# A two-block attention kernel: 64-row products padded to 128 rows, and x, meta tokens and norm weights also passed with features on the partitions

## The chip, the cores and the metric

The kernel runs on one core of a Trainium2 chip. The metric is the device time of one execution, in microseconds. Before the change it is 1644.33 us, the median of three runs (1641.67 to 1646.13).

## The reference

512 tokens of 2048 features pass through two blocks in float32. The first is sliding-window attention with sinks: 32 query heads of 64 share 4 key and value heads, each query sees 128 positions, and a learned bias by distance is added. Put short:

```
h = rms_norm(x, swa_norm);  q, k, v, gate = split(h @ w_in)          # 2048 x 4608
p = softmax with sink (q_norm . k_norm / 8 + bias, window 128)
x = x + ((p @ v) * silu(gate)) @ w_out
```

The second puts 16 meta tokens ahead of the sequence (528 positions) and runs two kinds of causal attention side by side, 8 heads each, on one normalised input. Differential heads ("d" in the code) have two 64-wide halves of q and k, a penalty linear in distance, and subtract one softmax from the other. Latent heads ("m") have q, k and v projected from narrow normalised latents plus a rotary part.

```
h = concat(meta_tokens, x);  proj = rms_norm(h, attn_norm_w) @ w_in
d: w = softmax(q0 k0' / 8 - slope*dist) - lam * softmax(q1 k1' / 8 - slope*dist);  o = rms_norm(w @ v)
m: o = softmax((q_nope k_nope' + q_pe k_pe') / sqrt(192)) @ v
h = h + (concat(o_d, o_m) * silu(gates)) @ w_out;  y = rms_norm(h, final_norm)[16:]
```

## The kernel before

Every large product is made at nearly float32 precision out of three float32r products: both operands are split into a rounded high part and the low rest, and high x high, high x low and low x high are accumulated in PSUM. ScalarE makes high parts (`wh` at L158, others in `split`, L268), VectorE the low ones (`wl` at L168, others at L272 and L274). Weights stream from HBM in 512 KB pieces (`Weights`, three raw buffers, up to four units of high and low parts ahead).

The work goes in stages: the first block's k and v projection (`kv_ps`, 16 steps over k, four token tiles each), its four q projections with attention pieces mixed in, its gates, its output projection; then the second block's latents, the heads, gates and output projection. In the head stage `Flow` counts units (three or so projection products each) and lets attention pieces in between: `s1` makes a block's scores, `norm` normalises, `s2` transposes the probabilities (L1304), `s2b` handles the last 16 columns of a block, `s3` multiplies by the values. There are 16 heads with four query blocks each.

The order of ScalarE, TensorE and VectorE is as written in the first k and v projection; later mostly ScalarE's alone (`phase({ACT})`), and a planner with its own cost estimates places the others. DMA issues, all on SyncE's queue, and GpSimd are always the planner's.

The first k and v projection needs x with features on the partitions. x is loaded with tokens on the partitions, in column blocks (`xc`), and `x_to_t` (L423) makes four TensorE transposes (L427) a step, after which `split` scales by the norm weight in `gcols` and rounds. `gcols`, 39 columns of norm weights, is itself made by transposing rows (`grow`). The sum of squares is taken by ScalarE (`squares`, L420), summed at k = 13 and turned into `rstd1` by two GpSimd operations (`rsqrt_mean`, L106 and L108); the evacuations of the four `kv_ps` banks (L549, L268, L274) need it. The next projection takes the same four banks. Ten warm-up transposes stand ahead of the transposes of x, and five behind the first four (L409).

In `s1` a differential head's scores are two products a half (L1253, L1254). The 128-row one pairs `dq` with the high and low parts of k stacked; the 64-row one adds the low part of q times the high part of k:

```
r = slice(64 * comp, 64 * comp + 64)
mm(o, qh[comp][:, qs], kh[comp][:, a:b], True, False)
mm(o, ql[r, qs], kh[comp][r, a:b], False, True)
```

`ql` is one tile (`dql`) whose upper half belongs to comp 0 and the lower to comp 1. Blocks 0 to 2 have one column range, block 3 has two. A latent head makes five 128-row products in the same place (`mqh`, `mql`, `mkh`, `mkl`, `qpt`, `kph`, `kpl`).

Because 528 positions are four tiles and 16 columns, each block's last 16 columns are collected in an edge tile of 64 rows (four blocks of 16). `s3` ends with three products over these 64 rows (L1342 to L1344: `pbh`, `pbl`, with the value rows `vh[:64, 4]`, `vl[:64, 4]`). The edge rows of the values come from products with 64 output rows (`mla_proj`) or from one transpose of 64 output rows (`te`, L1211), those of the probabilities from another (`edge`, L1323).

The second block's meta tokens are loaded as 16 rows and transposed by 16 products (`mps`, L847).

Of the kernel before, what the change touches and what calls it, by code (L numbers as in the profile page):

```python
# [9 lines left out]
F32 = mybir.dt.float32  # L10
# [8 lines left out]
KT = 16  # L19
# [16 lines left out]
def mixer_kernel(ctx, tc, x, rel_bias, swa_norm, w_in1, q_gain, k_gain, sinks, w_out1,  # L36
                 meta, attn_norm, w_in2, dlam, subln, qnorm, w_uq, kvnorm, w_ukv, w_out2,
                 fnorm, c_hot, c_out, c_rel, c_mask, c_cos, c_sin, out):
# [336 lines left out]
    def load_x(c, parts=1):  # L375
        t = xs.tile([128, NTB, 512], F32, tag="x", name="xcol", bufs=3)
        n = 512 // parts
        for i in range(parts):
            o = c * 512 + i * n
            nc.sync.dma_start(out=t[:, :, i * n:(i + 1) * n],  # L380
                              in_=x[:, o:o + n].rearrange("(t p) c -> p t c", p=128))
        return t

    grow = xs.tile([39, 128], F32, name="grow")

    def load_g(r, ap):
# [55 lines left out]
    def misc_a():  # L442
        for r, ap in ((16, attn_norm), (32, qnorm), (36, kvnorm), (38, subln)):
            load_g(r, ap)
# [15 lines left out]

    def misc_c():
        gps = tpt()
        nc.tensor.transpose(gps[:, 0, :39], grow, ident[:39, :39])
        nc.vector.tensor_copy(out=gcols[:, 16:39], in_=gps[:, 0, 16:39])
# [21 lines left out]
    for c in range(1, 3):  # L486
        xc.append(load_x(c))
# [6 lines left out]
    for k in range(KT):  # L494
# [5 lines left out]
        if k == 11:  # L500
            misc_c()
# [1089 lines left out]
```

## Time and profile before

| what | before |
|---|---|
| median of three runs | 1644.33 us |
| the profiled execution's own time / its span | 1643.65 / 1641.9 us |
| TensorE matmul busy, instructions | 1628.0 us (99%), 8674 |
| TensorE weight loads busy | 1373.1 us (84%) |
| VectorE / ScalarE / GpSimd busy | 906.9 (55%) / 731.8 (45%) / 86.5 (5%) us |
| mean granted TensorE clock | 0.999 |
| DMA | 173.65 MB, mean 106 GB/s |

PE is TensorE, PEld its weight loads, DVE VectorE, ACT ScalarE, POOL GpSimd, SPq the queue that issues the DMAs. In the timeline a row starts with its start and its duration in us, and rows of one kind that follow each other are merged (x4), their duration being that of all; a matmul's duration includes the pipeline's length, so rows overlap. A form such as `64*128 64x264` is a product over 64 rows with 128 output rows, moving 264 columns. A bracket at a row's end tells how long the engine sat idle before it and what ended that.

### The profile page before, as it was taken

How to read it: one execution, taken by the hardware profiler on the slowest of the kernel's cores; microseconds unless marked ns; L12 is line 12 of the kernel's file. 1: busy time of each engine (PE TensorE's matmuls, PEld its weight loads, DVE VectorE, ACT ScalarE, POOL GpSimd, SP SyncE). 2: the span in 40 equal slices, each digit the busy share in tenths (PEclk: the TensorE clock that was granted, in tenths of full speed). 3: DMA queues.
4: the chain of work that ended last, by engine and by line, in shares of the span. 5: the costliest groups of instructions: out<-in, count | busy, mean ns of one | idle time of the engine just before them, and what ended most of it. 6: DMA issues, size and time to landing. Idle time of an engine off the chain costs nothing.

```text
span 1641.9 us, 23349 instructions
## 1 busy us (share of the span) xinstructions
PE 1628.0 (99%) x8674; PEld 1373.1 (84%) x8674; DVE 906.9 (55%) x2220; ACT 731.8 (45%) x1624; POOL 86.5 (5%) x145
## 2 busy tenths in 40 slices
PE   9999999999999999999999999999999999999998
PEld 7888888887888888889898898898898788888887
DVE  4548888896444333333765656656556455455332
ACT  6456776774333332233554444444444333334222
POOL 0130320200000000000100000000000000000000
PEclk9999999999999999999999999999999999999999
DMA  7422323225434433333322222132132274355212
GB/s 226 134 86 81 104 85 99 81 59 176 125 94 126 159 117 137 103 119 81 84 75 71 65 82 75 56 84 71 55 90 71 72 224 123 96 218 180 91 51 103
DMA packets 145488, 173.65 MB, mean 106 GB/s; under 512 B 12967, under 2 KB 83406, under 8 KB 144846
## 3 DMA queue, kind: packets, MB, share of 16 engines
q1 hardware_dynamic: 145374, 172.16, 34.1%
q8 instruction: 68, 1.11, 0.3%
q14 instruction: 46, 0.38, 0.1%
HBM read 155.28 MB, written 16.84 MB: 105 GB/s over the span
## 4 chain that ended last, share of the span: by engine, by line
PE 94%; DVE 3%; ACT 2%; DMA 1%; issue 0%; POOL 0%; SPq 0%; ACTq 0%; POOLq 0%; DVEq 0%
PE pj L111 79%; PE sc L111 6%; PE pv L111 4%; PE tp L708 1%; PE tp L1304 1%; PE tp L427 1%; PE tp L636 1%; DMA oin<-ot_d 0%; PE sqs L1358 0%; PE ck_m L111 0%; ACT p L683 0%; DVE wl L168 0%; DMA xcol<-in_x_dram 0%; PE xtp L427 0%; DVE dk L272 0%
## 5 line engine op out<-in xcount | busy, mean ns | idle before, releaser
L168 DVE TENSOR_TENSOR wl<-raw,wh 128x512 fp32r<-128x512 f32 (+1 forms) x488 | 329.5, 682 | 421.4 <-ACT wh L158 419.3
L158 ACT ACTIVATE wh<-raw 128x512 fp32r<-128x512 f32 (+1 forms) x488 | 298.8, 619 | 405.6 <-PE pj L111 360.2
L111 PE MATMUL pj<-xh,wh 128*128 128x512 f32 (+1 forms) x1152 | 368.1, 356 | 0.0
L111 PE MATMUL pj<-xh,wl 128*128 128x512 f32 (+1 forms) x1152 | 356.5, 345 | 0.6 <-DVE wl L168 0.6
L111 PE MATMUL pj<-xl,wh 128*128 128x512 f32 (+1 forms) x1152 | 356.3, 345 | 0.0
L111 PEld LDWEIGHTS pj<-xh,wh 128*128 128x128 f32 x1152 | 204.7, 188 | 34.6 <-issue 3.1
L111 PEld LDWEIGHTS pj<-xh,wl 128*128 128x128 f32 x1152 | 199.7, 188 | 27.6 <-DVE wl L168 1.1
L111 PEld LDWEIGHTS pj<-xl,wh 128*128 128x128 f32 x1152 | 199.9, 188 | 19.7
L111 PE MATMUL pj<-wh,ogh 128*128 128x512 f32 (+1 forms) x528 | 205.0, 388 | 0.0
L111 PE MATMUL pj<-wh,ogl 128*128 128x512 f32 (+1 forms) x528 | 203.9, 386 | 0.0
L111 PE MATMUL pj<-wl,ogh 128*128 128x512 f32 (+1 forms) x528 | 203.8, 386 | 0.0
L111 PE MATMUL pj<-wh,xh 128*128 128x512 f32 (+1 forms) x448 | 176.8, 395 | 0.0
L111 PE MATMUL pj<-wh,xl 128*128 128x512 f32 (+1 forms) x448 | 171.2, 382 | 0.0
L111 PE MATMUL pj<-wl,xh 128*128 128x512 f32 (+1 forms) x448 | 170.8, 381 | 0.0
L1267 ACT ACTIVATE p2t<-p2t,nm 128x144 f32<-128x144 f32 (+3 forms) x96 | 55.2, 575 | 152.3 <-DVE nm L1263 152.2
L111 PEld LDWEIGHTS pj<-wh,ogl 128*128 128x128 f32 x528 | 99.3, 188 | 21.2
L111 PEld LDWEIGHTS pj<-wl,ogh 128*128 128x128 f32 x528 | 99.4, 188 | 20.6
L111 PEld LDWEIGHTS pj<-wh,ogh 128*128 128x128 f32 x528 | 99.3, 188 | 20.5
L111 PEld LDWEIGHTS pj<-wh,xl 128*128 128x128 f32 x448 | 84.4, 188 | 16.2
L111 PEld LDWEIGHTS pj<-wl,xh 128*128 128x128 f32 x448 | 84.7, 189 | 11.4
L111 PEld LDWEIGHTS pj<-wh,xh 128*128 128x128 f32 x448 | 84.5, 189 | 11.3
L683 ACT ACTIVATE p<-p,nm 128x256 f32<-128x256 f32 (+1 forms) x128 | 60.7, 476 | 60.6 <-DVE nm L679 60.5
(313 smaller groups left out, 2077.7 us busy)
## 6 DMA issues: line engine op xcount, KB each, us to landing
raw<-in_swa_w_in_dram SPq DMA_DIRECT2D x72, 512.0 KB, 3.6
raw<-in_w_in_dram SPq DMA_DIRECT2D x56, 512.0 KB, 3.7
raw<-in_swa_w_out_dram SPq DMA_DIRECT2D x32, 512.0 KB, 3.8
raw<-in_w_in_dram SPq DMA_DIRECT2D x128, 128.0 KB, 2.5
raw<-in_w_out_dram SPq DMA_DIRECT2D x32, 512.0 KB, 3.6
oin<-ot_d SPq DMA_DIRECT2D x8, 1024.0 KB, 7.3
bias<-bm_d SPq DMA_DIRECT2D x8, 512.0 KB, 5.3
ot_d<-ot SPq DMA_DIRECT2D x32, 128.0 KB, 1.8
```

Of the source, the lines that this page charges most:

```text
L111: nc.tensor.matmul(o, lhsT=l, rhs=r, start=start, stop=stop)
L158: nc.scalar.activation(out=h[:, :n], in_=self.raw_t[r][:, o:o + n], func=ACTF.Copy)
L168: nc.vector.tensor_tensor(out=l[:, :n], in0=self.raw_t[r][:, o:o + n], in1=f32(h[:, :n]), op=ALU.subtract)
L427: nc.tensor.transpose(tp[:, t, :], xcol[:, t, i * 128:(i + 1) * 128], ident)
L636: nc.tensor.transpose(tp[:, h, :].bitcast(F32R), qs[:, 4 * i + h].rearrange("p a b -> p (a b)"), identr)
L683: nc.scalar.activation(out=p[:, b, :w], in_=p[:, b, :w], func=ACTF.Exp, scale=-1.0, bias=nm[:, b:b + 1], accum_out=sm[:, b:b + 1])
L708: nc.tensor.transpose(tp[:, b, :], st[n]["p"][:, b, kb * 128:(kb + 1) * 128], ident)
L1267: nc.scalar.activation(out=p[:, :w], in_=p[:, :w], func=ACTF.Exp, scale=-1.0, bias=m, accum_out=sums[:, comp:comp + 1])
L1304: nc.tensor.transpose(tp[:, kb, :], p[:, kb * 128:(kb + 1) * 128], ident)
```

## The change

- Inputs: x is given a second time as `x_t` [2048, 512], the meta tokens as `meta_t` [128, 16, 16], and the five small norm weights as `gains` [128, 39]; the host lays them out. The row forms of the norm weights are no longer inputs.
- First k and v projection: `gcols` is one DMA. `x_t` is loaded into one tile `xt` in six pieces, four ahead of the loop and two at k = 1 and 2. `x_split(k)` scales and rounds out of SBUF; no transposes. `x_square(k)` squares on ScalarE and GpSimd adds up into `acc`; at k = 15 four products of `acc` with a column of ones give the sums. Warm-up: 30 transposes in a row.
- Meta tokens: `mps` is loaded, not transposed.
- Edges: all edge tiles have 128 rows or columns, zeros behind the 64. `ql` becomes two persistent tiles, each with one half zero, and all products in `s1`, `s3` and `mla_proj` take 128 rows.
- `dynamic_dma_scratch_size=4096` in the program's set-up.

```diff
-    def load_x(c, parts=1):
-        t = xs.tile([128, NTB, 512], F32, tag="x", name="xcol", bufs=3)
-        n = 512 // parts
-        for i in range(parts):
-            o = c * 512 + i * n
-            nc.sync.dma_start(out=t[:, :, i * n:(i + 1) * n],
-                              in_=x[:, o:o + n].rearrange("(t p) c -> p t c", p=128))
-        return t
-
-    grow = xs.tile([39, 128], F32, name="grow")
-
-    def load_g(r, ap):
-        n = ap.shape[1] // 128
-        nc.sync.dma_start(out=grow[r:r + n, :], in_=ap[0].rearrange("(k p) -> k p", p=128))
-
-    load_g(0, swa_norm)
-    xc = [xs.tile([128, NTB, 512], F32, tag="x", name="xcol", bufs=3)]
-    for i, (a, b) in enumerate(((0, 128), (128, 256), (256, 512))):
-        nc.sync.dma_start(out=xc[0][:, :, a:b], in_=x[:, a:b].rearrange("(t p) c -> p t c", p=128))
-        if i % 2 == 0:
-            W.load(i // 2)
+    nc.sync.dma_start(out=gcols, in_=gains)
+    xt = xs.tile([128, KT, S], F32, name="xt")
+
+    def load_xt(a, b):
+        nc.sync.dma_start(out=xt[:, a:b, :], in_=x_t[a * 128:b * 128, :].rearrange("(k p) c -> p k c", p=128))
+
+    load_xt(0, 1)
+    W.load(0)
+    load_xt(1, 2)
+    load_xt(2, 4)
+    W.load(1)
     W.nr = 2
+    load_xt(4, 7)
...
-    warm_up(10)
-    gps = tpt()
-    nc.tensor.transpose(gps[:, 0, :16], grow[:16], ident[:16, :16])
-    nc.vector.tensor_copy(out=gcols[:, 0:16], in_=gps[:, 0, :16])
-
-    ss1 = xs.tile([128, NTB, 4], F32, name="ss1")
+    warm_up(30)
+
+    acc = xs.tile([128, S], F32, name="acc")
+
+    def x_split(k):
+        split(xh1[:, k, :], xl1[:, k, :], xt[:, k, :], gcols[:, G1 + k:G1 + k + 1])
+
+    def x_square(k):
+
+        sq = acc if k == 0 else xs.tile([128, S], F32, tag="xsq", name="xsq", bufs=3)
+        nc.scalar.activation(out=sq, in_=xt[:, k, :], func=ACTF.Square)
+        if k:
+            nc.gpsimd.tensor_tensor(out=acc, in0=acc, in1=sq, op=ALU.add)
...
-    sq_done = set()
-    for c in range(1, 3):
-        xc.append(load_x(c))
-    x_to_t(xc[0], 0, 0, xh1, xl1, 0, G1)
+    x_split(0)
     W.high(0)
-    warm_up(5)
     F.run_posts()
     W.low(0)
-    x_to_t(xc[0], 0, 1, xh1, xl1, 0, G1, True)
+    x_split(1)
     for k in range(KT):
+        if k == 1:
+            load_xt(7, 12)
         if k == 2:
-            xc.append(load_x(3))
+            load_xt(12, 16)
             mi = misc_a()
         if k == 10:
             misc_b(*mi)
-        if k == 11:
-            misc_c()
         F.run_posts()
         W.get(c_kv, k)
         wh, wl = W.get(c_kv, k)
-        nx = k + 2
-        if 2 < nx < KT:
-            x_to_t(xc[nx // 4], nx // 4, nx % 4, xh1, xl1, 0, G1, nx % 2 == 1)
-        if 0 < k < 12:
-            for q in range(min(16, k * 4 // 3 + 2)):
-                if q not in sq_done:
-                    sq_done.add(q)
-                    squares(xc[q // 4], q // 4, ss1, xs, q % 4)
-        if k == 13:
+        if k + 2 < KT:
+            x_split(k + 2)
+        for q in range(KT):
+            if k > 0 and (k - 1) * 5 // 4 <= q < k * 5 // 4:
+                x_square(q)
+        if k == KT - 1:
+            ssp = ps_sc.tile([128, 512], F32, tag="sc", name="ssp")
+            for t in range(NTB):
+                nc.tensor.matmul(ssp[:, 2 * t:2 * t + 2], lhsT=acc[:, t * 128:(t + 1) * 128], rhs=ones2,
+                                 start=True, stop=True)
             ssr = xs.tile([128, NTB], F32, name="ssr")
-            nc.vector.tensor_reduce(out=ssr, in_=ss1, axis=AX.X, op=ALU.add)
+            nc.vector.tensor_copy(out=ssr, in_=ssp[:, 0:8].rearrange("p (a b) -> p a b", b=2)[:, :, 0])
             rsqrt_mean(rstd1, ssr, D)
...
-            if k == 0 and b == 1:
-                x_to_t(xc[0], 0, 2, xh1, xl1, 0, G1)
...
+        mps = xr_p.tile([128, KT, 16], F32, name="mps")
+        nc.sync.dma_start(out=mps, in_=meta_t)
...
-            mps = ps_tp.tile([128, KT, 16], F32, tag="tp", name="mps")
-            for k in range(KT):
-                nc.tensor.transpose(mps[:, k, :], mt[:, k * 128:(k + 1) * 128], ident[:16, :16])
...
-        CW = 2 * LK + 128
+        CW = 2 * LK + 256
         B2["ckh"] = ms.tile([128, CW], F32R, name="ckh")
         B2["ckl"] = ms.tile([128, CW], F32R, name="ckl")
+        for n_ in ("ckh", "ckl"):
+            nc.gpsimd.memset(f32(B2[n_][:, 2 * LK:]), 0.0)
...
-        B2["edge"] = [B2["p2"].tile([128, 64], F32, name=f"edge{i}") for i in range(2)]
-        for t in B2["edge"]:
+        B2["edge"] = [B2["p2"].tile([128, 128], F32, name=f"edge{i}") for i in range(2)]
+        B2["te"] = B2["p2"].tile([128, 128], F32, name="te")
+        B2["qlz"] = [B2["p2"].tile([128, S], F32R, name=f"dql{i}") for i in range(2)]
+        for t in B2["edge"] + [B2["te"]] + [f32(q) for q in B2["qlz"]]:
...
-                            c = slice(2 * LK + 64 * k, 2 * LK + 64 * k + 64)
+                            c = slice(2 * LK + 128 * k, 2 * LK + 128 * k + 128)
                             ah, al = B2["ckh"][:, c], B2["ckl"][:, c]
-                            o = o[:64]
...
-            ql = p2.tile([128, S], F32R, tag="dql", name="dql", bufs=1)
+            ql = B2["qlz"]
...
-                split(qd[i][half[i]], ql[half[i]], t[half[i], :S])
+                split(qd[i][half[i]], ql[i][half[i]], t[half[i], :S])
...
-                nc.tensor.transpose(tp[:64, 0, :], te, ident)
-                split(vh[:64, 4], vl[:64, 4], tp[:64, 0, :])
+                nc.tensor.transpose(tp[:, 0, :], te, ident)
+                split(vh[:, 4], vl[:, 4], tp[:, 0, :])
...
-                    r = slice(64 * comp, 64 * comp + 64)
                     mm(o, qh[comp][:, qs], kh[comp][:, a:b], True, False)
-                    mm(o, ql[r, qs], kh[comp][r, a:b], False, True)
+                    mm(o, ql[comp][:, qs], kh[comp][:, a:b], False, True)
...
-            nc.tensor.transpose(tp[:64, 0, :], pe, ident)
-            split(hd["pbh"], hd["pbl"], tp[:64, 0, :].rearrange("p (j c) -> p j c", j=4)[:, :, 16:32])
+            nc.tensor.transpose(tp[:, 0, :], pe, ident)
+            split(hd["pbh"], hd["pbl"], tp[:, 0, :].rearrange("p (j c) -> p j c", j=4)[:, :, 16:32])
...
-            mm(oc, vh[:64, 4, :], pbh, False, False)
-            mm(oc, vh[:64, 4, :], pbl, False, False)
-            mm(oc, vl[:64, 4, :], pbh, False, True)
+            mm(oc, vh[:, 4, :], pbh, False, False)
+            mm(oc, vh[:, 4, :], pbl, False, False)
+            mm(oc, vl[:, 4, :], pbh, False, True)
...
+def _columns(inputs):
+
+    import numpy as np
+    x_t = np.ascontiguousarray(np.asarray(inputs["x"])[0].T)
+    m = np.asarray(inputs["meta_tokens_2"])
+    meta_t = np.ascontiguousarray(m.reshape(META, KT, 128).transpose(2, 1, 0))
+    names = ("swa_norm", "attn_norm_w_2", "mla_q_norm_w_2", "mla_kv_norm_w_2", "diff_subln_w_2")
+    gains = np.concatenate([np.asarray(inputs[n])[0].reshape(-1, 128) for n in names])
+    return [("x_t", x_t), ("meta_t", meta_t), ("gains", np.ascontiguousarray(gains.T))]
...
-    nc = _bacc.Bacc("TRN2", target_bir_lowering=False, num_devices=1)
+    nc = _bacc.Bacc("TRN2", target_bir_lowering=False, num_devices=1, dynamic_dma_scratch_size=4096)
```

## Rows read from the trace of the kernel before

**Rows 1.** The page's chain that ended last, its shares by engine.

```profile
PE 94%; DVE 3%; ACT 2%; DMA 1%; issue 0%; POOL 0%; SPq 0%; ACTq 0%; POOLq 0%; DVEq 0%
```

**Rows 2.** Timeline of TensorE, latent scores: start us, duration us, engine, line, operation, names, form.

```profile
842.31 0.29 PE L111 MATMUL sc<-mkh,mql 128*128 128x264 f32 x1
842.43 0.29 PE L111 MATMUL sc<-kph,qpt 128*128 128x264 f32 x1
```

**Rows 3.** Timeline of all engines, the first projection's end.

```profile
57.73 0.39 PE L111 MATMUL pj<-wh,xh 128*128 128x512 f32 x1
...
58.67 0.47 ACT L549 ACTIVATE kn_all<-pj,rstd 128x256 f32<-128x256 f32 x1
...
59.60 0.48 DVE L274 SCALAR_TENSOR_TENSOR v<-pj,rstd,v 128x256 fp32r<-128x256 f32 x1 [0.31 <-ACT v L268]
...
60.45 0.39 PE L111 MATMUL pj<-wh,xh 128*128 128x512 f32 x1
```

**Rows 4.** Timeline of TensorE, one differential half.

```profile
863.61 0.28 PE L111 MATMUL sc<-dk,dq 128*128 128x272 f32 x1
863.83 0.39 PE L111 MATMUL sc<-dk,dql 64*128 64x272 f32 x1
864.15 0.50 PE L111 MATMUL pj<-xh,wh 128*128 128x512 f32 x1
864.48 0.39 PE L111 MATMUL pj<-xl,wh 128*128 128x512 f32 x1
```

**Rows 5.** View by tile, dql: count, durations min/median/max in ns, forms.

```profile
L111 PE MATMUL sc<-dk,dql x80: 379/387/449, 850.2 to 1297.3; 64*128 64x264 f32 x32, 64*128 64x256 f32 x16, 64*128 64x272 f32 x16, 64*128 64x400 f32 x16
```

**Rows 6.** Timeline of TensorE, end of one head's value sum.

```profile
866.27 0.28 PE L111 MATMUL pv<-pth,mvl 128*128 128x256 f32 x1
...
866.61 0.27 PE L111 MATMUL pv<-pbl,mvh 64*128 64x64 f32 x1
866.72 0.27 PE L111 MATMUL pv<-pbh,mvl 64*128 64x64 f32 x1
...
867.27 0.39 PE L111 MATMUL pj<-xl,wh 128*128 128x512 f32 x1
```

**Rows 7.** Timeline of TensorE, the meta tokens.

```profile
536.34 0.39 PE L111 MATMUL pj<-wh,ogl 128*128 128x512 f32 x1
536.65 1.16 PE L847 MATMUL mps<-identr,mt 16*128 16x16 f32 x16
537.74 0.50 PE L111 MATMUL pj<-wh,ogh 128*128 128x512 f32 x1
```

**Rows 8.** Timeline of TensorE, one step of the first projection.

```profile
24.98 0.60 PE L427 MATMUL xtp<-identr,xcol 128*128 128x128 f32 x4
...
28.17 0.60 PE L427 MATMUL tp<-identr,xcol 128*128 128x128 f32 x4
```

**Rows 9.** Timeline of all engines, the start.

```profile
1.63 2.39 PE L409 MATMUL pj<-identr 128*128 128x128 f32 x10 [1.63 <-DVE identr L404]
...
6.20 0.63 ACT L158 ACTIVATE wh<-raw 128x512 fp32r<-128x512 f32 x1 [0.19 <-DMA raw<-in_swa_w_in_dram]
...
7.82 0.78 PE L111 MATMUL pj<-wh,xh 128*128 128x512 f32 x1
...
8.39 0.63 PE L111 MATMUL pj<-wl,xh 128*128 128x512 f32 x1
...
10.10 0.43 PE L111 MATMUL pj<-wh,xl 128*128 128x512 f32 x1
```

**Rows 10.** View by windows: busy us (count) by engine, clock, DMA share, GB/s.

```profile
8.00:10.00 2.00, 2.00 (x6) 1.62 (x6) 1.08 (x2) 1.21 (x2) 0.00 (x0) 1.00 1.05 390
```

**Rows 11.** View by lines, GpSimd: busy us, mean ns, idle before.

```profile
L626 POOL TENSOR_TENSOR qn<-qn,st 128x512 f32<-128x512 f32 x16 | 17.8, 1111 | 1.3
...
L108 POOL TENSOR_TENSOR rstd<-rstd,mhalf 128x4 f32<-128x4 f32 x2 | 2.0, 1020 | 0.2
```

**Rows 12.** View by lines and forms, TensorE: busy us, mean ns, idle before, releaser.

```profile
L1304 PE MATMUL tp<-identr,p2t 128*128 128x128 f32 x160 | 28.1, 274 | 0.9 <-DVE p2t L1283 0.6
```

More of the change, by code (lines that the diff above doesn't have):

```diff
@@ L35, in mixer_kernel @@
 @with_exitstack
-def mixer_kernel(ctx, tc, x, rel_bias, swa_norm, w_in1, q_gain, k_gain, sinks, w_out1,
-                 meta, attn_norm, w_in2, dlam, subln, qnorm, w_uq, kvnorm, w_ukv, w_out2,
-                 fnorm, c_hot, c_out, c_rel, c_mask, c_cos, c_sin, out):
+def mixer_kernel(ctx, tc, x, rel_bias, w_in1, q_gain, k_gain, sinks, w_out1,
+                 meta, w_in2, dlam, w_uq, w_ukv, w_out2, fnorm,
+                 x_t, meta_t, gains, c_hot, c_out, c_rel, c_mask, c_cos, c_sin, out):
     nc = tc.nc
@@ L442, in misc_a @@
     def misc_a():
-        for r, ap in ((16, attn_norm), (32, qnorm), (36, kvnorm), (38, subln)):
-            load_g(r, ap)
         srow = xs.tile([128, 32], F32, name="srow")
@@ L459, in misc_a @@
         return srow, gq_t, gk_t, relt, hot, outm, lrow
[L461 to L464, printed above, removed]
     def misc_b(srow, gq_t, gk_t, relt, hot, outm, lrow):
@@ L1018, in edges @@
             for nm_ in ("ckh", "ckl"):
-                e = B2[nm_][:, 2 * LK + 64 * k:2 * LK + 64 * k + 64]
+                e = B2[nm_][:, 2 * LK + 128 * k:2 * LK + 128 * k + 64]
                 nc.vector.tensor_copy(out=e.rearrange("p (j c) -> p j c", j=4),
@@ L1142, in mla_proj @@
                     F.unit()
-                n = 128 if b0 < 4 else 64
-                split(vh[:n, b0:b0 + nb].rearrange("p a b c -> p (a b c)"),
-                      vl[:n, b0:b0 + nb].rearrange("p a b c -> p (a b c)"), pv[:n, :nb * 256])
+                split(vh[:, b0:b0 + nb].rearrange("p a b c -> p (a b c)"),
+                      vl[:, b0:b0 + nb].rearrange("p a b c -> p (a b c)"), pv[:, :nb * 256])
         vh, vl = heads["v"]
@@ L1215, in ev @@
             F.defer(3, tr2)
-            te = p2.tile([128, 64], F32, tag="te", name="te", bufs=1)
+            te = B2["te"]
             F.post(lambda: nc.vector.tensor_copy(
-                out=te.rearrange("p (j c) -> p j c", j=4), in_=edge(t)))
+                out=te[:, 0:64].rearrange("p (j c) -> p j c", j=4), in_=edge(t)))
         proj_t(c_dv[h], KT, [(slice(0, 128), [(pk[i][:, :HALF], hv[i]) for i in range(2)], ev)])
@@ L1292, in s2 @@
                     ptl=p2.tile([128, PTW], F32R, tag="ptl", name="ptl2", bufs=1),
-                    pbh=p2.tile([64, 4, 16], F32R, tag="pbh", name="pbh", bufs=1),
-                    pbl=p2.tile([64, 4, 16], F32R, tag="pbl", name="pbl", bufs=1))
+                    pbh=p2.tile([128, 4, 16], F32R, tag="pbh", name="pbh", bufs=1),
+                    pbl=p2.tile([128, 4, 16], F32R, tag="pbl", name="pbl", bufs=1))
             hd = st[kind, h]
@@ L1578 @@
     from concourse.bass_utils import run_bass_kernel_spmd as _run
-    nc = _bacc.Bacc("TRN2", target_bir_lowering=False, num_devices=1)
+    nc = _bacc.Bacc("TRN2", target_bir_lowering=False, num_devices=1, dynamic_dma_scratch_size=4096)
     arrays, args = {}, []
-    pairs = [(n, _np.ascontiguousarray(inputs[n])) for n in _INS] + _constants()
+    pairs = [(n, _np.ascontiguousarray(inputs[n])) for n in _INS] + _columns(inputs) + _constants()
     for name, a in pairs:
```

5 lines of the change are left out of this document (2 added, 3 removed).

## The prediction

> **What bounds the kernel now.** I read the chain of waits first: TensorE holds nearly all of it [rows 1], so the span is the sum of what TensorE does, and other engines count only where TensorE waits for them. Its busy time says little here, because matmuls are pipelined and a row's duration overlaps the next one. The price of a product is its slot: from its own start to the start of the next row in the timeline. A 264-column product of 128 rows takes 0.12 us [rows 2]; twelve 512-column products take 2.72 us (57.73 to 60.45), 0.23 each [rows 3]. The reader should look for places where a slot is longer than the column count explains. There are three kinds, and the change touches them all.
>
> **The 64-row score products.** In a differential head each block of scores is a 128-row product (dq) and a 64-row product (dql). The stretch dq, dql, next projection product takes 0.87 us, 863.61 to 864.48 [rows 4]. At full-row prices it would be 0.12 + 0.12 + 0.23, with a trifle for 272 columns: 0.48. The excess is 0.39: the slot before the 64-row product is 0.22 instead of 0.12, its own 0.32 instead of 0.12, the one after it 0.33 instead of 0.23. The latent heads make five 128-row products in a row beside the same projections, and their slots are the plain 0.12 [rows 2]; so what is dear is going into 64 rows and out again. The change gives ql 128 rows, one half of them zero. There are 80 such products [rows 5]: 80 x 0.39 = 31.2 us off the path. Columns and weights loaded stay as they are. Bounds: at best all 31.2; at worst nothing, if the slot belongs to these operands and not to the row count. I take 31.2, since the nearest full-row products of the same width show no excess.
>
> The Trainium skill speaks against it (TensorE: Matmul & The Clock Gate, "Why this matters for your kernels"): a small-K product takes the same time as a 128-row one, and the gain lies in running several at once on distinct row groups. By that the padding is worth nothing, and the sum is some 6 us. The trace disagrees, with 0.32 against 0.12 for the slot. It is a rival below.
>
> **The 64-row edge products.** Each of 16 heads ends its sum of probabilities by values with three 64-row products of 64 columns. From the last 128-row product ahead of them to the second product behind, 866.27 to 867.27, are 1.00 us [rows 6]. Plain: 0.12 for 256 columns, 0.23 for 512, and three times 0.11, the slot of the middle one (866.61 to 866.72), which changes no mode: 0.68. Excess 0.32; I take 0.31, as some are followed by shorter products: 16 x 0.31 = 5.0 us. Bounds 0 and 5.1. Products whose output has 64 rows (the value edges, the transposes of te and edge) also become 128 wide. Their moving columns don't change, so I take nothing; if the wider weight load showed, it would be at most half of a 0.11 slot for each of 24 transposes, 1.3 us. The new zero fills lie on GpSimd, idle there, once, under projection products ahead of the first head's scores.
>
> **Meta tokens.** Sixteen transposes of 16 rows go: 536.65 to 537.74 is 1.09 us, the slot ahead of them is 0.31 instead of 0.23 [rows 7], and leaving the mode costs 0.10 as in rows 4. That is 1.3 us. The transfer that replaces them is issued 20 units ahead of its use.
>
> **The first projection.** x arrives with features on the partitions, so 16 groups of four transposes go. One step over k takes 3.19 us with a group, 24.98 to 28.17 [rows 8], and 2.72 without [rows 3]: 0.47 a group. Fourteen lie behind the slow start: 6.6 us. The first two belong to the start, which I price as a whole.
>
> The start: the first projection product begins at 7.82, four slots of 0.43 run from 8.39 to 10.10 [rows 9], and later ones take 0.23 [rows 3]. TensorE runs at the lower of its two levels, 1.2 GHz, in that stretch, although the view by windows gives 1.00 for its clock [rows 10]. After the change the first product needs the first weights, rounded at 6.20 + 0.63 = 6.83 [rows 9], and the end of thirty warm-up transposes instead of fifteen. Ten take 2.39 us [rows 9], so thirty end near 8.0 at the lower level. If the clock doesn't rise in them, the first product starts 0.2 late and its half-speed successors cost the 1.1 us of before: about zero. If it rises in them, products start at 6.9 at full speed; less 0.4 for VectorE's first low half, 1.7 us are won. If it rises 3 us later than now, 1.7 are lost. I take zero, since the fifteen transposes did not raise it before the products came.
>
> The Trainium skill has the same of transposes (TensorE: Matmul & The Clock Gate, Part 4): they don't count as busy in the same way; by it the upper end, 1.7 us won, falls away. No run here shows thirty without a pause.
>
> Transfers: the first pass takes x and weights of 4.2 MB each, and TensorE needs 16 x 2.72 = 44 us for it; a full queue moves 390 GB/s [rows 10], 22 us for both. The weights for k = 6, with all the x queued ahead of them, are 5.2 MB, 14 us of transfer, wanted some 23 us into the span. No loss.
>
> The sum of squares moves from accumulating activations to plain squares on ScalarE and 15 adds on GpSimd at 1.11 us [rows 11], 17 us beside 35 us of products: hidden. But its last step moves to the beginning of k = 15: four tiny products on TensorE (priced as four slots of 0.11 and one change of mode at 0.08: 0.5), a copy, then the power on GpSimd, 1.02 us [rows 11]; with the small operation ahead of it and the handovers some 2.0 from the last product's step. The first evacuation now begins 0.94 after the step's start (58.67 against 57.73) and frees its bank at 59.60 + 0.48 = 60.08, 0.37 ahead of the next projection at 60.45 [rows 3]. After the change it begins about 2.0 after that start, 1.06 later: TensorE waits 0.7. Behind it on ScalarE are the other seven evacuations and weight halves that are three units ahead; the second bank is wanted six products later, with over a microsecond to spare. Loss 0.5 + 0.7. The stage wins 6.6 - 1.2 = 5.4 us, with the start's bounds 3.7 to 7.1.
>
> **What is late next.** Shorter scores leave VectorE and ScalarE less time before the transposes of the probabilities. TensorE sits idle ahead of these for 0.9 us in all 160 now [rows 12]. At worst one in four of the 64 query blocks loses a saved 0.39: 6.2 us; at best none. I take 1.5, near the present 0.9.
>
> **Sum.** 31.2 + 5.0 + 1.3 + 5.4 - 1.5 = 41.4. The profiled execution took 1643.65 us (span 1641.9 and 1.75 around it): 1602.2. It lies 0.7 under the median of the runs, 1644.33; I forecast 1602.5.
>
> **Rivals.**
> 1. The padded products keep their long slots. Only meta tokens and the first stage pay, 1.3 + 5.4: 1637. For it: dq and dql alternate operands. Against: so do the latent scores, at 0.12. Chance 0.05.
> 2. The softmax chain takes half of the 36 us of scores and edges back, because transposes then wait for the normalisation: 1620. For it: one releaser, the normalisation, ended 0.6 of the 0.9 us [rows 12]. Against: that is small over 160. It decides from 0.3 us a block. Chance 0.10.
> 3. Slower: in the attention stage only ScalarE keeps the written order, so the planner may place VectorE's normalisation so late that the transposes of every one of the 64 blocks wait for it. From 42.9 / 64 = 0.67 us a block the gain is gone; at 0.8 the time is 1643.65 - 42.9 + 51.2 = 1652. For it: waits of this kind exist [rows 12]. Against: the change adds nothing to VectorE's chain there, so a wait can mostly only return what was saved. Chance 0.03.
>
> The forecast has the remaining 0.82.
>
> **Numbers.** The forecast's own range: the start 1.7 either way, edge transposes 1.3, returned waits up to 4.7 more, another order by the planner some 2: 1597 to 1612. With a little of rival 2's side the range is 1596 to 1614. A difference of 0.3%, 5 us, is what can be told from none. Faster: the forecast and rivals 1 and 2 but for 0.02: 0.95; same 0.02; slower 0.03.
>
> **What would show it.** Right: slots of dq and dql both 0.12; the first projection at 2.7 us a step and its end near 55; under 1 us of waiting ahead of the second projection; more idle time ahead of the transposes of the probabilities. Wrong: padded products with 0.3 us slots; TensorE idle on x or weights in the first 30 us; blocks whose transposes wait regularly.

## The result, and the profile after

| | before | after |
|---|---|---|
| median of four runs each, us | 1643.51 (1641.67 to 1646.13) | 1604.52 (1603.41 to 1606.12) |
| ratio to before, 95% interval | | 0.9762 (0.9745 to 0.9779) |
| profiled execution, us | 1643.65 | 1604.56 |
| its span, us | 1641.9 | 1602.8 |

Of the executions below, one (of the run with the later broadcast) took 7605.23 us and is left out. The forecast was 1602.5 us, in a range from 1596 to 1614. The time lies 2.0 us above it. To find where that comes from, I cut both spans at the same points of the written order (the first product of each stage), so that every stage has its own difference:

| stage | before | after | won | forecast |
|---|---|---|---|---|
| span's start to the first projection's first product | 7.82 | 6.47 | 1.35 | 0 (with the slow slots behind it) |
| first projection, to the second one's first product | 52.64 | 49.81 | 2.83 | 5.4 |
| first output projection, with the meta tokens (to its last three products) | 185.55 | 185.09 | 0.46 | 1.3 |
| first to last dql product | 447.11 | 413.12 | 33.99 | |
| last dql to the second output projection | 161.11 | 160.52 | 0.59 | |
| the last two lines together (the heads) | | | 34.58 | 31.2 + 5.0 - 1.5 = 34.7 |
| all other stages together | | | -0.1 | 0 |

The heads came as forecast; the first projection and the meta tokens gave less.

**The whole.** The chain that ended last by engine, of after [rows 1]:

```profile
PE 91%; DVE 4%; ACT 2%; DMA 1%; issue 1%; POOL 0%; SPq 0%; ACTq 0%; POOLq 0%; DVEq 0%
```

TensorE still sets the end. Its share falls by three points, which is more than the 39 of 1642 us that went: the chain now passes through VectorE in more places. Which waits became longer is read stage by stage below.

**The score products.** TensorE's timeline over one differential half of after [rows 4]; columns as there:

```profile
852.33 0.29 PE L111 MATMUL sc<-dk,dq 128*128 128x272 f32 x1
852.46 0.29 PE L111 MATMUL sc<-dk,dql 128*128 128x272 f32 x1
852.58 0.39 PE L111 MATMUL pj<-xh,wh 128*128 128x512 f32 x1
852.81 0.40 PE L111 MATMUL pj<-xl,wh 128*128 128x512 f32 x1
```

The view by tile, dql [rows 5]:

```profile
L111 PE MATMUL sc<-dk,dql x80: 278/284/349, 845.8 to 1258.9; 128*128 128x264 f32 x32, 128*128 128x256 f32 x16, 128*128 128x272 f32 x16, 128*128 128x400 f32 x16
```

From dq to the second projection product are 0.48 us now, 0.87 before. The reader should compare starts, not durations: dql's own duration fell by only 0.1 us, its slot by 0.20.

**The edges.** TensorE's timeline at the end of one head's value sum [rows 6]:

```profile
860.37 0.28 PE L111 MATMUL pv<-pth,mvl 128*128 128x256 f32 x1
860.48 0.19 PE L111 MATMUL pv<-pbh,mvh 128*128 128x64 f32 x1
860.51 0.27 PE L111 MATMUL pv<-pbl,mvh 128*128 128x64 f32 x1
...
860.73 0.48 PE L111 MATMUL pj<-xh,wh 128*128 128x512 f32 x1
861.05 0.39 PE L111 MATMUL pj<-xl,wh 128*128 128x512 f32 x1
```

0.68 us from the first to the last of these rows, 1.00 before. That is the figure worked out in the prediction, but its terms are not: the first edge product's slot is 0.03 and not 0.11, and the projection product behind takes 0.32 and not 0.23. That the two deviations cancel in this head is luck.

**The transposes of the probabilities.** View by lines and forms [rows 12]:

```profile
L1290 PE MATMUL tp<-identr,p2t 128*128 128x128 f32 x160 | 28.0, 273 | 1.9 <-DVE p2t L1269 1.9
```

The idle time ahead of them rose from 0.9 to 1.9 us, with the same releaser. That is rival 2's mechanism, at a thirty-sixth of what was saved.

**The meta tokens.** Timeline of all engines around their normalisation [rows 7]:

```profile
531.90 1.90 ACT L831 ACTIVATE mjunk<-mt 16x2048 f32<-16x2048 f32 x1
...
533.97 0.18 POOL L106 TENSOR_SCALAR mrstd<-mss 16x1 f32<-16x1 f32 x1 [223.31 <-ACT mjunk L831]
...
534.24 0.81 POOL L108 TENSOR_TENSOR mrstd<-mrstd,mhalf 16x1 f32<-16x1 f32 x1
...
535.11 0.39 PE L432 MATMUL rbps<-identr,mrstd 16*128 16x16 f32 x2 [0.75 <-POOL mrstd L108]
```

The sixteen transposes are gone, but the next thing on TensorE in that unit broadcasts a reciprocal root. Its chain (the squares on ScalarE, two small operations on GpSimd) takes over three microseconds, and the transposes used to run beside its squares (536.65 to 537.74, the squares 535.90 to 537.80). Now TensorE sits idle for 0.75 us.

**The start.** TensorE's timeline [rows 9]:

```profile
1.63 5.08 PE L400 MATMUL pj<-identr 128*128 128x128 f32 x30 [1.63 <-DVE identr L395]
6.47 0.48 PE L111 MATMUL pj<-wh,xh 128*128 128x512 f32 x1
7.09 0.49 PE L111 MATMUL pj<-wl,xh 128*128 128x512 f32 x1
7.42 0.39 PE L111 MATMUL pj<-wh,xl 128*128 128x512 f32 x1
7.65 0.40 PE L111 MATMUL pj<-wh,xh 128*128 128x512 f32 x1
```

Thirty transposes took 5.08 us, where ten alone took 2.39 before: they sped up on the way. The trace's record of the granted clock has the upper level from 4.92 us on, in the midst of the transposes and ahead of any product (10.16 before). From 7.42 on the slots are 0.23, none is 0.43. The second product waits for VectorE's first low half of the weights, which runs from 6.34 to 7.03 in this trace.

**Weights that come late.** Timeline of all engines, 25 to 27 us:

```profile
25.20 0.63 ACT L158 ACTIVATE wh<-raw 128x512 fp32r<-128x512 f32 x1 [3.10 <-DMA raw<-in_swa_w_in_dram]
...
25.73 0.71 ACT L268 ACTIVATE xh<-xt,gcols 128x512 fp32r<-128x512 f32 x1
...
25.85 0.39 PE L111 MATMUL pj<-wh,xl 128*128 128x512 f32 x1
...
26.50 0.50 PE L111 MATMUL pj<-wh,xh 128*128 128x512 f32 x1 [0.26 <-ACT xh L268]
```

And SyncE's queue of the same kernel, which issues the loads:

```profile
18.06 0.35 SPq L454 DMA_DIRECT2D lrow<-in_diff_lambda_dram  x1
21.16 8.18 SPq L140 DMA_DIRECT2D raw<-in_swa_w_in_dram  x4
```

The weights of the fifth load are issued at 21.16, behind seven small loads. ScalarE waits 3.10 us for them, and the high half of x that stands behind them in its order is late for TensorE. Slots of 0.65 at 25.85 and 0.45 at 26.84 stand where 0.23 is plain. Before the change the same load was issued at 21.16 too and landed even later, at 28.30; it was rounded at 28.40, where the trace names a TensorE product as what ended ScalarE's wait. So the load isn't later than before; TensorE is earlier.

The queue itself moved on as earlier transfers landed: its issues at 16.70, 18.06 and 21.16 follow landings of earlier loads at 16.69, 18.04 and 21.10. Meanwhile the transfers ran dry: from 21 to 22 us the DMA engines were busy 0.20 of the time, at 53 GB/s.

**Two engines that block each other.** Timeline of all engines, the next stretch:

```profile
27.52 1.43 DVE L168 TENSOR_TENSOR wl<-raw,wh 128x512 fp32r<-128x512 f32 x1 [0.29 <-ACT wh L158]
...
28.76 1.35 POOL L414 TENSOR_TENSOR acc<-acc,xsq 128x512 f32<-128x512 f32 x1 [0.37 <-ACT xsq L412]
...
28.87 1.79 DVE L274 SCALAR_TENSOR_TENSOR xl<-xt,gcols,xh 128x512 fp32r<-128x512 f32 x1
...
30.42 1.39 POOL L414 TENSOR_TENSOR acc<-acc,xsq 128x512 f32<-128x512 f32 x1 [0.31 <-ACT xsq L412]
...
30.58 1.78 DVE L168 TENSOR_TENSOR wl<-raw,wh 128x512 fp32r<-128x512 f32 x1
...
30.72 0.50 PE L111 MATMUL pj<-wh,xl 128*128 128x512 f32 x1 [0.42 <-DVE xl L274]
```

VectorE's low halves take 0.69 and 0.75 us alone; here they take 1.43 to 1.79. Add start and duration: GpSimd's rows end at 30.11 and 31.81, and the VectorE rows that began within them at 30.66 and 32.36, each 0.55 later. In turn the GpSimd rows end 1.16 and 1.15 us after the VectorE rows that were running when they began (28.95 and 30.66). Read so, the two don't share: each stands still until the other is done. GpSimd's spans are rough in a profile, but the pattern is regular: every one of the stage's 13 slow VectorE rows ends 0.55 us after the GpSimd row it met, and all 15 GpSimd rows end 1.14 to 1.18 us after the VectorE row they met. Of the stage's 36 VectorE rows of these lines, 13 are over 1 us (none before), and TensorE waits for low halves at 29.91, 33.34 and 48.63 (slots 0.81, 0.77, 0.73).

The Trainium skill has this (SBUF — State Buffer, "Who interferes with whom"): a VectorE instruction with two inputs in SBUF contends with a GpSimd instruction that reads SBUF, and whichever issues second blocks until the first is done. The trace agrees, with the 0.55 us. I had priced the adds from a GpSimd row alone and did not weigh this rule.

**The bank between the projections.** Timeline of all engines, the first projection's end [rows 3]:

```profile
52.23 0.47 PE L500 MATMUL ssp<-ones,acc 128*128 128x2 f32 x3
...
54.81 0.47 ACT L535 ACTIVATE kn_all<-pj,rstd 128x256 f32<-128x256 f32 x1 [2.23 <-POOL rstd L108]
...
55.20 0.39 PE L111 MATMUL pj<-wh,xl 128*128 128x512 f32 x1
...
55.74 0.48 DVE L274 SCALAR_TENSOR_TENSOR v<-pj,rstd,v 128x256 fp32r<-128x256 f32 x1 [2.35 <-ACT v L268]
...
56.28 0.50 PE L111 MATMUL pj<-wh,xh 128*128 128x512 f32 x1 [0.69 <-DVE v L274]
```

This is the wait that the prediction put at 0.7. The slot from 55.20 to 56.28 is 1.07 us instead of 0.23, so 0.85, and 0.11 more go with the next slot (0.34). After such a wait the product's weight load no longer lies ahead of it: at 26.49 it starts 0.01 before its product, at 8.12 in plain flow 0.23 before.

The sums themselves cost more than was priced. The four products written for them are eight rows in the trace and hold TensorE from 51.76 to 52.57, 0.81 us, and the slot behind them is 0.32 instead of 0.23.

### The profile page after: what moved, and what is told of

Read it like the earlier page. It is cut to its first block, busy times and chain, and to the rows that moved or that the text cites. A ratio compares the mean times of both kernels' runs of the same rounds, so it can differ in the third digit from the quotient of the medians.

```text
span 1602.8 us, 23242 instructions
## 1 busy us (share of the span) xinstructions
PE 1585.7 (99%) x8615; PEld 1358.8 (85%) x8615; DVE 917.8 (57%) x2218; ACT 727.9 (45%) x1608; POOL 110.1 (7%) x165
## 4 chain that ended last, share of the span: by engine, by line
PE 91%; DVE 4%; ACT 2%; DMA 1%; issue 1%; POOL 0%; SPq 0%; ACTq 0%; POOLq 0%; DVEq 0%
PE pj L111 78%; PE sc L111 4%; PE pv L111 4%; PE tp L694 1%; PE tp L1290 1%; DMA xt<-in_x_t_dram 1%; DVE wl L168 1%; PE tp L622 1%; PE tp L425 0%; DVE xl L274 0%; PE sqs L1344 0%; PE ck_m L111 0%; ACT p L669 0%; DVE dql L272 0%; ACT wh L158 0%
## 5 line engine op out<-in xcount | busy, mean ns | idle before, releaser
L168 DVE TENSOR_TENSOR wl<-raw,wh 128x512 fp32r<-128x512 f32 (+1 forms) x488 | 336.0, 695 | 404.9 <-ACT wh L158 403.0
L111 PE MATMUL pj<-xh,wh 128*128 128x512 f32 (+1 forms) x1152 | 363.6, 352 | 0.0
```

The lines of the kernel that those rows point to most:

```text
L111: nc.tensor.matmul(o, lhsT=l, rhs=r, start=start, stop=stop)
L168: nc.vector.tensor_tensor(out=l[:, :n], in0=self.raw_t[r][:, o:o + n], in1=f32(h[:, :n]), op=ALU.subtract)
```

## The experiments

Times are medians; a ratio is to the kernel before, measured beside it. "After" is 1604.52 us, 0.9762. Four runs touch the heads, five the first stage or the meta tokens, and the last puts the mendings together.

### One part back: 64-row scores

```diff
-                    mm(o, ql[comp][:, qs], kh[comp][:, a:b], False, True)
+                    r = slice(64 * comp, 64 * comp + 64)
+                    mm(o, ql[comp][r, qs], kh[comp][r, a:b], False, True)
```

> The changed kernel with one line back: the low score product of a differential half is taken over its 64 rows again, out of the same padded tiles, with the same operands, columns and order. Theory A (it is the change between 128 and 64 rows that costs, 0.39 us for each of 80 products): 1604.5 + 31, less about 1 that the waits before the transposes gave back, so 1634 to 1636, and slots of about 0.22, 0.32 and 0.33 us around such a product. Rival (the long slots belong to the operands or to their tiles, and fell for another reason): 1604 to 1607, slots of 0.12.

Measured: 1634.65 us, 0.9945 (0.9931 to 0.9960), 30.1 above after. The tile's view:

```profile
L111 PE MATMUL sc<-dk,dql x80: 379/387/450, 845.6 to 1288.5; 64*128 64x264 f32 x32, 64*128 64x256 f32 x16, 64*128 64x272 f32 x16, 64*128 64x400 f32 x16
```

With 64 rows alone the durations of before are back, and the stage from the first to the last dql is 442.83 us instead of 413.12. The operands alternate as they do in after, so the long slots belong to the row count. Rival 1 falls.

### One part back: 64-row edges

```diff
-            mm(oc, vh[:, 4, :], pbh, False, False)
-            mm(oc, vh[:, 4, :], pbl, False, False)
-            mm(oc, vl[:, 4, :], pbh, False, True)
+            mm(oc, vh[:64, 4, :], pbh[:64], False, False)
+            mm(oc, vh[:64, 4, :], pbl[:64], False, False)
+            mm(oc, vl[:64, 4, :], pbh[:64], False, True)
```

> The changed kernel with the three edge products of each head taken over 64 rows again, out of the same padded tiles. Theory A: 16 heads x 0.31 us = 5 us more, 1609 to 1610, with the slot ahead of the group at 0.21 and the last of it at 0.20 us. Rival (edge products cost the same either way): 1604 to 1605.

Measured: 1609.99 us, 0.9796 (0.9782 to 0.9811), 5.5 above after; the stage of the heads is 4.6 longer. TensorE's timeline:

```profile
861.05 0.29 PE L111 MATMUL pv<-pbh,mvh 64*128 64x64 f32 x1
861.18 0.27 PE L111 MATMUL pv<-pbl,mvh 64*128 64x64 f32 x1
861.30 0.27 PE L111 MATMUL pv<-pbh,mvl 64*128 64x64 f32 x1
861.50 0.51 PE L111 MATMUL pj<-xh,wh 128*128 128x512 f32 x1
861.84 0.40 PE L111 MATMUL pj<-xl,wh 128*128 128x512 f32 x1
```

Slot by slot against the full-row rows of after: the product ahead 0.21 instead of 0.11, the first edge product 0.13 instead of 0.03, the middle one 0.12 instead of 0.11, the last 0.20 instead of 0.11, the projection product behind 0.34 instead of 0.32. What costs is leaving the mode and entering it, not being in it.

### The padding alone

The kernel before with the padding of scores and edges, and neither the new x nor the new meta tokens. Its core:

```diff
-                    r = slice(64 * comp, 64 * comp + 64)
...
-                    mm(o, ql[r, qs], kh[comp][r, a:b], False, True)
+                    mm(o, ql[comp][:, qs], kh[comp][:, a:b], False, True)
...
-            mm(oc, vh[:64, 4, :], pbh, False, False)
+            mm(oc, vh[:, 4, :], pbh, False, False)
```

> The kernel before with the padding alone (scores, edges, their tiles), x and the meta tokens as before. Theory A: the head stage falls by 34 to 35 us as in the changed kernel and no other stage moves by more than 0.3 us, so 1643.5 - 34.5 = 1609. Rival (a part of the 34 us comes from the planner's other order after a shorter first stage): 1612 to 1620.

Measured: 1609.87 us, 0.9794 (0.9779 to 0.9808), 34.2 under the 1644.08 of the kernel before beside it. The heads' stage is 413.10 us, that of after to 0.02. So the padding gives seven eighths of the gain (34.2 of 39.0).

This kernel also has the start of the kernel before, instruction for instruction. Its timeline there [rows 9]:

```profile
8.67 0.48 PE L111 MATMUL pj<-wh,xh 128*128 128x512 f32 x1
8.99 0.40 PE L111 MATMUL pj<-wl,xh 128*128 128x512 f32 x1
```

The first products are 0.32 and 0.23 apart, not 0.57 and 0.43: here the clock rose at 6.56, ahead of any product, where the same instructions had it rise at 10.16 in the kernel before. I had read that one profile as a rule.

### Two 64-row products at once

For blocks 0 to 2 the two halves' low products stand next to each other, one on the upper, one on the lower 64 rows, in two banks; block 3 stays padded.

```diff
...
+                for c in range(2):
+                    r = slice(64 * c, 64 * c + 64)
+                    mm(st[n]["sc"][c][0][:, :b - a], ql[c][r, qs], kh[c][r, a:b], False, True)
...
```

> The changed kernel with 64-row low products for blocks 0 to 2 of the differential heads, but both halves' products one right behind the other, on the upper and the lower 64 rows, into two banks; block 3 keeps the padded form. 24 pairs replace 48 padded products of 0.12 us. If one round trip into 64 rows and back is paid a pair, and the two run one after the other: 24 x 0.39 = 9.4 us more, 1614. If the two run at once beside that round trip: 24 x 0.27 = 6.5 us more, 1611. If each pays its own: 18.7 us more, 1623. The Trainium skill's rule for products on distinct row groups, run at once (TensorE: Matmul & The Clock Gate, Why this matters for your kernels), taken without a price for going into 64 rows, gives 24 x 0.12 = 2.9 us less, 1601.6.

Measured: 1610.49 us, 0.9803 (0.9789 to 0.9816), 6.0 above after. TensorE's timeline, one row for the pair:

```profile
859.02 0.28 PE L111 MATMUL sc<-dk,dq 128*128 128x272 f32 x1
859.24 0.39 PE L111 MATMUL sc<-dk,dql 64*128 64x272 f32 x2
859.56 0.50 PE L111 MATMUL pj<-xh,wh 128*128 128x512 f32 x1
859.90 0.39 PE L111 MATMUL pj<-xl,wh 128*128 128x512 f32 x1
```

The two start 3 to 4 ns apart and are over in one row's 0.39 us: they run at once, as the Trainium skill says they do (TensorE: Matmul & The Clock Gate, "Why this matters for your kernels"). The three slots, 0.22, 0.32 and 0.34, are those of a single 64-row product [rows 4]. So the pair costs one trip into the mode and out, 0.39 us, and saves one full-row slot of 0.12; alone among 128-row products it loses: 24 x 0.27 = 6.5 us by these slots, 6.0 in the time and in the stage. The Trainium skill (TensorEngine Tiling (Array Packing), "Key Properties") says that a change of mode drains TensorE; the longer slots agree with that, at 0.39 us there and back.

### GpSimd's adds left out

This kernel leaves 15 of the 16 squares out of the sum, so its first normalisation is incomplete.

```diff
         nc.scalar.activation(out=sq, in_=xt[:, k, :], func=ACTF.Square)
-        if k:
-            nc.gpsimd.tensor_tensor(out=acc, in0=acc, in1=sq, op=ALU.add)
```

> The changed kernel without the 15 GpSimd adds that sum the squares of x (the squares are made, only the first is used, so the first normalisation is left incomplete). Theory B (GpSimd's adds slow VectorE's two-operand work beside them, so low halves of x come late and TensorE waits): VectorE's L168 and L274 rows fall from 1.4 to 1.8 us back to 0.7 in the first projection, and the waits at 29.9, 33.3 and 48.6 us (0.5 us each) go; 1.5 to 2.5 us less, about 1602.5. Rival C (these waits come from weights that landed late at 25.1 us, and VectorE would have caught up): the rows fall, the waits stay within 0.5 us in all, 1604 to 1605. Both: the bank wait of 0.85 us ahead of the second projection stays.

Measured: 1604.14 us, 0.9761 (0.9746 to 0.9776). The first projection falls from 49.81 to 46.75 us, and no VectorE row of its two lines is over 1 us. TensorE's waits for low halves at 29.91, 33.34 and 48.63 have no counterpart (one of 0.2 for the late weights is left, at 27 us); the bank's wait is unchanged (slot 1.08). The median shows almost nothing of these 3.1 us, where 1.5 to 2.5 were expected. The profiled execution shows 1.7 (1602.83 against 1604.56): its first product started at 7.79 instead of 6.47, as the clock rose only at 7.62, near the end of the thirty transposes. The stage answers, the time of the whole doesn't.

### The adds on VectorE, a step later

```diff
-            nc.gpsimd.tensor_tensor(out=acc, in0=acc, in1=sq, op=ALU.add)
+            sums.append(sq)
...
+            nc.vector.tensor_tensor(out=acc, in0=acc, in1=sums.pop(), op=ALU.add)
```

> The changed kernel with the 15 adds on VectorE, each one step after its square, instead of GpSimd. Theory B (the two engines slow each other): VectorE's L168 and L274 rows stay at 0.7 us, an add takes 0.7, VectorE has about 2.1 us of work in a step of 2.7, and the waits for low parts mostly go; 1 to 2.5 us less than 1604.5. Rival C (VectorE's load is the bound, wherever the adds are): the waits stay or grow, 1604.5 or more.

Measured: 1603.35 us, 0.9756 (0.9740 to 0.9773); first projection 48.65. VectorE's timeline:

```profile
19.49 0.68 DVE L413 TENSOR_TENSOR acc<-acc,xsq 128x512 f32<-128x512 f32 x1
20.09 0.75 DVE L274 SCALAR_TENSOR_TENSOR xl<-xt,gcols,xh 128x512 fp32r<-128x512 f32 x1
```

The add takes VectorE 0.68 us; beside GpSimd's add each low half lost up to 1.1. No row is slow, and the waits for low halves at 30, 33 and 49 us are gone. The stage fell by only 1.2 us, because the waits for the late weights grew (slots 0.79 and 1.04 at 25.83 and 26.96, where after has 0.65 and 0.45): they came 0.12 later, and behind them the add now stands ahead of a low half that TensorE waits for.

### The weights ahead of the small loads

```diff
-            mi = misc_a()
...
+        if k == 4:
+            mi = misc_a()
```

> The changed kernel with the seven small loads (sinks, gains, bias table and its two masks, lambda) issued at k = 4 instead of k = 2, so that the fifth pair of weights isn't queued behind them. Theory C (each of them waits on SyncE's queue for an earlier transfer to land, and the weights for k = 8 are issued at 21.2 instead of some 12 us): the weights' transfer is issued before 17 us and lands by 23, and the waits for x's high part at 25.9 and for its low part at 26.8 us (0.65 us together with their after-effects) go; 0.6 to 1.5 us less. Theory B: the waits at 29.9, 33.3 and 48.6 us stay, since the adds are still there.

Measured: 1603.63 us, 0.9757 (0.9741 to 0.9774); first projection 48.32. SyncE's queue:

```profile
11.61 0.37 SPq L140 DMA_DIRECT2D raw<-in_swa_w_in_dram  x1
```

The fifth weights are issued at 11.61 instead of 21.16 and land at 22.41 instead of 25.09. Of the two waits near 26 us one is left, of 0.18. For low halves TensorE waits twice, at 44 and 47 us (slots 0.44 and 0.78), instead of three times; the blocking stayed (14 slow rows).

### Ten transposes instead of thirty

```diff
-    warm_up(30)
+    warm_up(10)
```

> The changed kernel with 10 warm-up transposes instead of 30. In the changed kernel TensorE's granted clock rose at 4.92 us, in the midst of the transposes; before the change it rose at 10.16 us, after fifteen transposes with pauses and 2.3 us of products. Theory D (transposes without a pause raise the clock as products do, and a pause puts it off): with ten, TensorE stands idle from 4 to 6.4 us, the first products run at half speed (slots of 0.43), and the clock rises only after 8 us; 0.8 to 2 us more. Rival (the transposes have no part in it, the clock rises at a time of its own): it rises near 5 us again, slots are 0.23 from the first product on, no difference.

Measured: 1605.13 us, 0.9765 (0.9751 to 0.9780). TensorE's timeline:

```profile
6.22 0.79 PE L111 MATMUL pj<-wh,xh 128*128 128x512 f32 x1 [2.19 <-ACT wh L158]
...
7.54 0.63 PE L111 MATMUL pj<-wh,xl 128*128 128x512 f32 x1
7.96 0.63 PE L111 MATMUL pj<-wh,xh 128*128 128x512 f32 x1
```

I expected the loss at the start to be seen in the time. The half-speed slots are there (0.43 from 7.54 to 9.24, the clock up at 9.57), but the second projection begins at 56.03, 0.25 earlier than in after: the slow slots bring TensorE 1.0 us later to the product that waits in after, and it no longer waits (no long slot near 26 us). In this profile a faster start is worth nothing, since the next load decides.

### The broadcast of the meta tokens eight units later

```diff
-            row_bcast(rb2[:, 0:16], mrstd, 16)
+            F.defer(8, lambda: row_bcast(rb2[:, 0:16], mrstd, 16))
```

> The changed kernel with the broadcast of the meta tokens' norm put off by 8 units. In the changed kernel TensorE waits 0.8 us for it at 533.96 us, where the sixteen transposes had covered the chain of square, power and broadcast. Theory E: that wait goes and nothing else changes, 0.8 us less, visible in the stage and at the limit of what times tell. Rival: the wait moves to the next thing that needs the same buffers, no gain.

Measured: 1603.71 us (1603.39 to 1605.86, three executions), 0.9762 (0.9745 to 0.9778). TensorE's timeline:

```profile
540.42 0.39 PE L432 MATMUL rbps<-identr,mrstd 16*128 16x16 f32 x2
```

The wait is gone, and the stage takes 184.27 us instead of 185.09. The median is 0.8 us lower, as expected, but the executions scatter by more than that. The profiled one (1605.86) doesn't show the gain: there the fifth weights landed at 26.42, and one slot at 25.94 is 1.88 us long.

### All four mended

The weights ahead of the small loads, the adds on VectorE, the broadcast later, and the squares at three in two steps, so that the sum of squares stands at k = 13 instead of 15:

```diff
-            if k > 0 and (k - 1) * 5 // 4 <= q < k * 5 // 4:
+            if k > 0 and (k - 1) * 3 // 2 <= q < k * 3 // 2:
...
-        if k == KT - 1:
+        if k == 13:
```

> The changed kernel with the small loads at k = 4, the adds on VectorE, the squares half a step faster so that the sums are made at k = 13 instead of 15, and the meta tokens' broadcast 8 units later. Theory F (late weights, GpSimd's adds beside VectorE, the late sum and the meta broadcast each cost their own waits): the first projection's waits of 1 us and 0.5 us go, it takes 46 us from its first product instead of 49.8, the bank wait of 0.85 us goes, the meta stage is 0.8 us shorter: 1604.5 - 3.8 - 0.8 = 1599 to 1600.5. Rival (another operand is late as soon as these are on time, ScalarE having 2.3 us of work in a step of 2.7): 1601.5 to 1603.

Measured: 1600.73 us (1599.91 to 1602.45), 0.9745 (0.9732 to 0.9758), the fastest of all kernels here, and 0.2 above the range expected. The first projection's last product and the second's first one:

```profile
52.46 0.39 PE L111 MATMUL pj<-wh,xl 128*128 128x512 f32 x1
52.69 0.39 PE L111 MATMUL pj<-wh,xh 128*128 128x512 f32 x1
```

0.23 apart: no wait for the bank. The stage is 45.56 us, 4.25 less than in after, and none of its slots is a wait for x or weights. The first output projection is 184.25. Here the first product started at 7.12, 0.65 later than in after. The single changes left the bank's slot at 1.08, so it is the earlier sums that remove it.

## Why the prediction was right, and where it missed

**Score products, 31.2.** Right. The slots of dql, of dq and of the product behind them sum to 30.9 us less than before (15.5, 9.7 and 5.7); the experiment that puts 64 rows back costs 30.1. The Trainium skill's rule on small-K products (TensorE: Matmul & The Clock Gate, "Why this matters for your kernels"), weighed there, gives them the time of a 128-row product. Inside the mode the trace agrees (the middle edge product's slot is 0.12 at 64 rows and 0.11 at 128), but not for a lone one: the rule leaves out the change of mode.

**Edges, 5.0.** Right in size: from the full-row product ahead to the projection product behind, the slots sum to 5.0 us less over the 16 heads; the experiment gives 4.6 in the stage and 5.5 in the time. The plain price inside it was put together from slots that do not hold one by one, as told above. The wider outputs cost nothing that a row shows (the transposes of te and edge take 0.27 before and after).

**What is late next, 1.5.** Right in kind, 1.0 in size [rows 12].

**Meta tokens, 1.3.** Mis-sized: 0.46. The step counted what left TensorE's queue and didn't ask what those sixteen transposes had covered. The broadcast's chain (1.90 + 0.18 + 0.81 us and the handovers) was the next thing late. Moving the broadcast gave 0.82 us of stage back, so the two together are the 1.3 of the forecast.

**The first projection, 5.4 with the start at 0.** 4.2 came (1.35 + 2.83), from terms of which several were wrong. That the stage came out within 1.2 us is luck: a gain at the start that was put at nothing paid for more than half of the losses that were put at nothing.
- The start. I chose the middle, because fifteen transposes had not raised the clock before. In after it rose during the thirty, and the start gave 2.0, above the upper bound of 1.7: the first product came 1.35 earlier, and 0.7 less went in long slots (1.2 over the first six before, 0.5 now). In all nine profiles with thirty the clock rose between 4.4 and 7.6 us, ahead of the first product. But with the fifteen of before it rose once at 10.16, behind products, and once at 6.56, ahead of them, so the number of transposes is not shown to be what decides; with ten it rose at 9.57. What sets the moment is open. The Trainium skill's sentence on transposes and the clock, cited in that step, is not borne out: in ten of these profiles the clock rose with nothing but transposes run.
- "Transfers: ... No loss." This step failed. It summed bytes against the rate of a full queue, and the bytes up to the fourth weights do fit. But the fifth weights stood behind seven small loads on SyncE, and its queue moved on only as earlier transfers landed. 0.9 us, with the longer slots behind the waits. That the order on SyncE has this part is shown by the experiment that changes only that order; its loads then land 2.7 us earlier, behind x, and 0.3 of the 0.9 is left (slots 0.40 and 0.34). The prediction's own sign of being wrong, TensorE idle on x or weights in the first 30 us, is there.
- "15 adds on GpSimd ...: hidden." This step failed too. GpSimd's time was hidden; what it did to VectorE was not. Three waits for low halves, 2.0 us. Both experiments that take the adds from GpSimd end the slow rows and these waits.
- The sums: 0.9 for 0.5, since the products are eight and not four.
- The bank: 0.85, and 0.11 behind it in the next stage, for 0.7. The chain is the one that was worked out, and earlier sums remove it.
- One gain had no term: the 39-row transpose of the other norm weights (45.17 before the change) went from this stage too, 0.3 with the longer slot ahead of it.

In sum: 2.0 (start) + 6.6 (transposes) + 0.3 (the other norm weights) - 0.9 (sums) - 0.9 - 2.0 - 0.85 = 4.25, near the 4.2 that came.

**Rivals.** 1 fell with the 64-row scores. 2's mechanism is there at 1 us. 3 has no trace: no block's transposes wait regularly.

**Open.** In single profiles the first product starts between 6.3 and 7.8 us in kernels with the same warm-up, and the fifth weights land at different times. Among after and the four single mendings the times therefore don't decide; their stages do, each read from one profile. How far that carries is seen in the five profiles whose first stage is the same (after, the 64-row scores, the 64-row edges, the pairs and the later broadcast): the first projection takes 49.25 to 50.60 us and the second one begins at 56.28 to 57.60. The kernels without GpSimd's adds, with earlier weights, and with the adds on VectorE lie below all of these (46.75, 48.32 and 48.65; 54.53, 54.72 and 54.96), but the exact worth of each is not known better than that scatter. The other stages repeat much better: the stage of the heads takes 413.04 to 413.12 us in eight profiles.

## What to carry to other kernels

A lone 64-row product among 128-row ones costs a trip into another mode and out, 0.39 us or three times a full-row slot here; filling its operand with zeros was cheaper, and even a pair that runs at once didn't pay for the trip. When work leaves the engine that sets the end, ask of each neighbour what that work was covering: the next load, the next chain of small operations and the next bank are each wanted earlier by what was saved. "Idle engine" is not a price: here an add on idle GpSimd that reads SBUF stopped VectorE's operations with two SBUF inputs, and in this stage 0.68 us on VectorE itself was cheaper.

## What the runs showed of the hardware that was not expected

- The clock rose to its upper level with only transposes run, at moments that differ between runs of the same instructions (6.56 and 10.16 us for one start, 4.4 to 7.6 for the other).
- VectorE with two inputs in SBUF and GpSimd adding in SBUF take strict turns: each slow VectorE row ends 0.55 us after GpSimd's, 0.69 us becomes 1.43 to 1.78.
- After TensorE has stood idle for an operand, the next slot is 0.34 instead of 0.23, so each wait costs 0.11 beyond its own long slot.
- The mode's price does not grow with the products that lie inside: 0.39 us around one dql and around a pair, 0.32 around three edge products.
